# Decoder trunk on one core: softmax sums of a head's two attention units in one tile, guard on GpSimd, first query blocks turned together

## The chip, the cores and the metric

The kernel runs on one core of a Trainium2 chip. A core has five engines that run their own instruction streams and meet at semaphores: TensorE (in the profile PE, with its weight loads as PEld), VectorE (DVE), ScalarE (ACT), GpSimd (POOL) and SyncE (SP), which here issues the DMAs. The metric is the device time of one execution in microseconds; the median of three runs is 2022.24 us (2020.12 to 2023.56).

## The reference, cut to what matters

Two layers over 512 positions of width 1024, each a half-step SwiGLU, a token mixer, and another half-step SwiGLU, all with modulated norms. Layer 0's mixer is a short convolution beside latent attention with 8 heads. Layer 1's is sparse attention with 16 heads in three branches: compressed blocks, selected blocks, sliding window. With 512 positions the selection takes all 8 blocks and the window all positions, so that both branches are plain causal attention over 512 positions, each with its own keys and values:

```
def masked_softmax(s, mask):
    s = where(mask, s, NEG_INF)
    m = max(s, axis=-1)
    p = exp(s - m) * mask
    return p / maximum(sum(p, axis=-1), 1e-20)
...
o = gate0 * o_compressed + gate1 * o_selected + gate2 * o_window   # per head
```

The floor of 1e-20 under the sum is what this document calls the guard. The tensors are f32; products run as sums of products of a rounded high part and its remainder (`split`).

## The kernel before, in words

One program, unrolled: norms, feed-forward nets, and the two mixers one after another. The instructions of every engine stand in an order that a planner fixes when the program is built: it takes the order of the source as priority and lets an instruction pass others of its engine when, by its own costs, those aren't ready yet. At run time each engine's queue keeps that order, and an instruction whose operands are not ready holds what stands behind it.

Both mixers call `attend` (L512) with a list of units. A unit is one causal attention over 512 queries and keys: in layer 0 a head (8 units, `ahead=1`), in layer 1 a branch of a head (32 units; the selected branch has `ahead=2`, the window branch `ahead=0`). The queries of a unit go in four blocks of 128; block i sees (i+1) x 128 keys.

- `scores(n, i)` (L525): TensorE makes the scores of block i of unit n. VectorE adds the mask and takes the minimum in one operation (L547; the scores carry the opposite sign), with an operation that reads out the minimum. ScalarE exponentiates in place and sums (L549), with one that reads out the sum. After block 1 and after block 3, for the two blocks last made: the guard on the sums (L552, VectorE, 128x2), the reciprocal (L553, VectorE), and for each of the two blocks a multiplication by reciprocal and gate in place on GpSimd (L557). With `ahead=2` one pair of products makes block 0 of this unit and of the next, and the next unit then has no block 0 of its own. Minima, sums and reciprocals lie in a tile of four columns for each unit.
- `turn(n, i)` (L559): TensorE transposes block i (L565), and `split` puts the high part (ScalarE, L100) and the remainder (VectorE, L101) into `h`. Even units have the tiles 0 to 7 of `h`, odd units 8 to 15 (`ptile`, L856).
- `values(n)` (L569): the products of probabilities and values, into a bank of their own (L574); a unit that is the last of its head folds the two halves (L603, L604).

In pass n the loop at L580 calls: hook, scores(n, 0), scores(n, 1), turn(n-1, 0), scores(n, 2), turn(n-1, 1), values(n-2), scores(n, 3), turn(n-1, 2), turn(n-1, 3). The hook of layer 1 spreads the compressed branch over the passes, a quad of four heads at a time (L1048 to L1073), which is the period of the stage. `e` (blocks 1 to 3 of a unit) has two buffers, `e0` four, PSUM banks of tag A six.

Of the kernel before, what the change touches and what calls it, by code (L numbers as in the profile page):

```python
# [12 lines left out]
AF = mybir.ActivationFunctionType  # L13
OP = mybir.AluOpType
# [3 lines left out]
P = 128  # L18
# [12 lines left out]
class Net:  # L31
# [480 lines left out]
    def attend(self, units, hook, beside=iter(())):  # L512

        nc = self.nc
        live = {}

        def scores(n, i):  # L525
            u = units[n]
            w = (i + 1) * P
            qk, ahead = u["qk"], 1
            if i == 0:
                qk, ahead = u["first"] or qk, u["ahead"]  # L530
                for k in range(ahead):
                    live[n + k] = dict(e0=u["e0"](), mn=self.small(4), sum=self.small(4), r=self.small(4))
                if not ahead:
                    return
            L = live[n]
            if i == 1:
                L.update(e=u["e"](), pt=u["pt"](n))
            s = self.bank()
            for p, (q, k) in enumerate(qk):
                k = k[..., :w]  # L540
                nc.tensor.matmul(s[:, :ahead * w], q[:, i * P:(i + 1) * P], k, start=(p == 0),  # L541
                                 stop=(p == len(qk) - 1))
            for k in range(ahead):
                L = live[n + k]
                e = self.eblk(L, i)
                mn = L["mn"][:, i:i + 1]
                nc.vector.tensor_tensor_reduce(e, s[:, k * w:(k + 1) * w], self.cmask[:, S - w:], 1.0, 3e38, OP.add,  # L547
                                               OP.min, accum_out=mn)
                nc.scalar.activation(e, e, AF.Exp, bias=mn, scale=-1.0, accum_out=L["sum"][:, i:i + 1])  # L549
            if i % 2:  # L550
                c = slice(i - 1, i + 1)
                nc.vector.tensor_scalar(L["sum"][:, c], L["sum"][:, c], 1e-20, None, op0=OP.max)  # L552
                nc.vector.reciprocal(L["r"][:, c], L["sum"][:, c])  # L553
                for b in (i - 1, i):
                    g = 1.0 if u["gate"] is None else u["gate"](b)
                    eb = self.eblk(L, b)
                    nc.gpsimd.tensor_scalar(eb, eb, L["r"][:, b:b + 1], g, op0=OP.mult, op1=OP.mult)  # L557

        def turn(n, i):  # L559
            L = live[n]  # L560
            e = self.eblk(L, i)
            b = self.bank()
            w = (i + 1) * P
            for kb in range(i + 1):
                nc.tensor.transpose(b[:, kb * P:(kb + 1) * P], e[:, kb * P:(kb + 1) * P], self.ident)  # L565
            hi, lo = (t[:, 0:i + 1, i * P:(i + 1) * P] for t in L["pt"])
            self.split(b[:, :w].rearrange("p (k q) -> p k q", q=P), hi, lo)

        def values(n):  # L569
            u, L = units[n], live.pop(n)  # L570
            y, first = u["y"]()
            for kb in range(4):
                for p, t in enumerate(L["pt"]):
                    nc.tensor.matmul(y[:, kb * P:], u["v"](kb), t[:, kb, kb * P:], start=(first and kb == 0 and p == 0),  # L574
                                     stop=(u["last"] and kb == 3 and p == 1))
            if u["last"]:
                u["done"](y)

        N = len(units)
        for n in range(N + 2):  # L580
            hook(n)
            for i in range(5):
                if n < N and i < 4:
                    scores(n, i)
                if (n, i) in ((0, 1), (0, 3), (1, 1)):
                    next(beside, None)
                if 1 <= n <= N and i > 0:
                    turn(n - 1, i - 1)
                if n >= 2 and i == 2:
                    values(n - 2)  # L590

    def eblk(self, L, i):
        if i == 0:
# [632 lines left out]
```

## Time and profile before

| | |
|---|---|
| median of three runs | 2022.24 us (2020.12 to 2023.56) |
| the profiled execution: time, span | 2022.17 us, 2020.4 us |
| TensorE busy (granted clock 0.994 in the mean) | 1969.8 us, 97% |
| weight loads | 1659.3 us, 82% |
| VectorE busy | 1137.5 us, 56% |
| ScalarE busy | 765.7 us, 38% |
| GpSimd busy | 204.7 us, 10% |
| DMA | 248.06 MB, mean 123 GB/s |

The shares are means over stages with different limits. TensorE's busy time is modelled from pipelined instructions, so a TensorE that is busy all the time isn't one at its peak. The layer 0 attention lies at about 500 to 565 us, the layer 1 attention at about 1437 to 1597 us. The views below are the busy times by stretches, the groups by line and shape, the timeline, the waits, and the chain of waits that ended last.

### The profile page before, as it was taken

Reading aid. Unit: us, or ns where it says so; the run is one execution under the profiler, and the core shown is the slowest. Engines: PE = TensorE matmul, PEld = TensorE weight load, DVE = VectorE, ACT = ScalarE, POOL = GpSimd, SP = SyncE. Lnnn points to the kernel's source line nnn. Section 1 sums busy time; section 2 is a strip of 40 time slices with the busy share of each in tenths; the row PEclk is TensorE's granted clock in tenths of the full one; section 3 lists DMA queues with packets and bytes.
Section 4 is the critical chain, followed back from the end, with each engine's and each line's share of the span. In section 5 each row is a group of like instructions: output and inputs, shape, how many; then the busy total and the mean of one; then the engine's idle time right before and its main releaser. Section 6 shows DMA issues by size and latency. Waiting matters only on the chain. (4 is left out here: it accounts for less than half of the span.)

```text
span 2020.4 us, 26114 instructions
## 1 busy us (share of the span) xinstructions
PE 1969.8 (97%) x9990; PEld 1659.3 (82%) x9990; DVE 1137.5 (56%) x1993; ACT 765.7 (38%) x1372; POOL 204.7 (10%) x388
## 2 busy tenths in 40 slices
PE   6999999999999999999999999999999999999998
PEld 5788888897789888888988888889777798888887
DVE  7756566268756666663545443356799753333332
ACT  3322322245844223222422222236688643222223
POOL 3000000022400000000100000020355310000000
PEclk8999999999999999999999999999999999999999
DMA  9646666343114566664346452334200023333231
GB/s 277 195 134 206 190 205 206 84 100 94 43 53 126 177 193 206 192 207 139 108 122 177 126 153 87 96 97 119 62 1 2 22 74 115 94 95 99 88 97 49
DMA packets 374434, 248.06 MB, mean 123 GB/s; under 512 B 23207, under 2 KB 356262, under 8 KB 374310
## 3 DMA queue, kind: packets, MB, share of 16 engines
q1 hardware_dynamic: 373440, 245.24, 41.2%
q8 instruction: 78, 1.28, 0.3%
q10 hardware_dynamic: 870, 1.16, 0.2%
q14 instruction: 46, 0.38, 0.1%
HBM read 244.28 MB, written 2.10 MB: 122 GB/s over the span
## 5 line engine op out<-in xcount | busy, mean ns | idle before, releaser
L100 ACT ACTIVATE wh<-wr 128x1024 fp32r<-128x1024 f32 (+2 forms) x317 | 328.5, 1037 | 926.2 <-PE psA L126 388.0
L101 DVE TENSOR_TENSOR wl<-wr,wh 128x1024 fp32r<-128x1024 f32 (+2 forms) x317 | 379.7, 1200 | 396.4 <-ACT wh L100 390.6
L126 PE MATMUL psA<-h,wh 128*128 128x512 f32 (+1 forms) x1312 | 488.1, 372 | 1.0 <-DVE h L386 1.0
L127 PE MATMUL psA<-h,wl 128*128 128x512 f32 (+1 forms) x1312 | 488.6, 373 | 0.0
L125 PE MATMUL psA<-h,wh 128*128 128x512 f32 (+1 forms) x1312 | 485.0, 374 | 2.9 <-DVE mod L221 1.6
L126 PEld LDWEIGHTS psA<-h,wh 128*128 128x128 f32 x1312 | 247.4, 189 | 46.5 <-DVE h L386 1.7
L125 PEld LDWEIGHTS psA<-h,wh 128*128 128x128 f32 x1312 | 246.4, 189 | 46.6 <-issue 1.7
L127 PEld LDWEIGHTS psA<-h,wl 128*128 128x128 f32 x1312 | 247.2, 188 | 43.7
L125 PE MATMUL psY<-h,wh 128*128 128x512 f32 (+2 forms) x568 | 209.0, 368 | 0.0
L126 PE MATMUL psY<-h,wh 128*128 128x512 f32 (+2 forms) x568 | 208.5, 367 | 0.0
L127 PE MATMUL psY<-h,wl 128*128 128x512 f32 (+2 forms) x568 | 208.4, 367 | 0.0
L125 PE MATMUL psA<-g,wh 128*128 128x512 f32 (+1 forms) x528 | 192.7, 365 | 0.0
L126 PE MATMUL psA<-g,wh 128*128 128x512 f32 (+1 forms) x528 | 191.9, 363 | 0.0
L127 PE MATMUL psA<-g,wl 128*128 128x512 f32 (+1 forms) x528 | 191.6, 363 | 0.0
L279 DVE SCALAR_TENSOR_TENSOR acc<-wr,cact,acc 128x1024 f32<-128x1024 f32 x112 | 143.6, 1283 | 73.2 <-DMA wr<-in_ada_w 71.8
L351 POOL TENSOR_SCALAR s<-s 128x2 int32<-128x2 int32 (+1 forms) x14 | 5.1, 366 | 1534.1 <-ACT s L350 1534.0
L126 PEld LDWEIGHTS psY<-h,wh 128*128 128x128 f32 (+1 forms) x568 | 106.1, 187 | 18.5
L125 PEld LDWEIGHTS psY<-h,wh 128*128 128x128 f32 (+1 forms) x568 | 106.3, 187 | 18.1
L127 PEld LDWEIGHTS psY<-h,wl 128*128 128x128 f32 (+1 forms) x568 | 106.2, 187 | 17.9
L127 PEld LDWEIGHTS psA<-g,wl 128*128 128x128 f32 x528 | 99.7, 189 | 15.6
L126 PEld LDWEIGHTS psA<-g,wh 128*128 128x128 f32 x528 | 99.7, 189 | 15.5
L125 PEld LDWEIGHTS psA<-g,wh 128*128 128x128 f32 x528 | 99.7, 189 | 15.3
(274 smaller groups left out, 2596.5 us busy)
## 6 DMA issues: line engine op xcount, KB each, us to landing
wr<-in_ff_w SPq DMA_DIRECT2D x234, 512.0 KB, 4.6
wr<-in_ada_w SPq DMA_DIRECT2D x128, 512.0 KB, 4.2
wr<-in_ff_w SPq DMA_DIRECT2D x40, 384.0 KB, 3.0
ar<-in_ada_w SPq DMA_DIRECT2D x16, 512.0 KB, 5.8
wr<-in_hy_w_in SPq DMA_DIRECT2D x15, 512.0 KB, 3.9
wr<-in_nsa_w_in SPq DMA_DIRECT2D x14, 512.0 KB, 3.8
wr<-in_hy_w_out SPq DMA_DIRECT2D x8, 512.0 KB, 5.9
wr<-in_nsa_w_out SPq DMA_DIRECT2D x8, 512.0 KB, 3.6
```

The source lines that it names most:

```text
L100: nc.scalar.activation(hi, src, AF.Copy)
L101: (lo_eng or nc.vector).tensor_tensor(lo, src, hi.bitcast(F32), op=OP.subtract)
L125: mm(out, lh, rh, start=first, stop=False)
L126: mm(out, lh, rl, start=False, stop=False)
L127: self.product = mm(out, ll, rh, start=False, stop=last).ins
L279: nc.vector.scalar_tensor_tensor(acc, raw, self.cact[:, k:k + 1], acc, op0=OP.mult, op1=OP.add)
L351: pool.tensor_scalar(y.bitcast(I32), ms.bitcast(I32), -0.5, float(0x5F3759DF), op0=OP.mult, op1=OP.add)
```

## The change

- With `ahead=2` the two units of a head share tiles of eight columns for minima, sums and reciprocals. Block b of the first unit has column b + 1; of the second unit block 0 has column 0 and block b column b + 4.
- Guard, reciprocal and multiplications follow a table. In the sparse attention there are three runs a head: after block 1 of the first unit for its blocks 0 and 1 and the second unit's block 0 (columns 0 to 2); after block 3 of the first unit for its blocks 2 and 3; after block 3 of the second unit for its blocks 1, 2 and 3. The latent attention keeps its two runs a unit.
- The guard is issued on GpSimd, in both attentions.
- In the sparse attention the two first blocks of a head are transposed into one bank in the pass after the first unit's, and split with one copy and one subtraction into the tiles of both units.
- `values(n - 2)` stands ahead of `turn(n - 1, 0)` in pass n, after scores(n, 1), in both attentions.

```diff
@@ -528,8 +528,13 @@
             qk, ahead = u["qk"], 1
             if i == 0:
                 qk, ahead = u["first"] or qk, u["ahead"]
-                for k in range(ahead):
-                    live[n + k] = dict(e0=u["e0"](), mn=self.small(4), sum=self.small(4), r=self.small(4))
+                if ahead == 2:
+
+                    sh = {q: self.small(8, tag=q) for q in ("mn", "sum", "r")}
+                    live[n] = dict(sh, e0=u["e0"](), col=lambda b: b + 1)
+                    live[n + 1] = dict(sh, e0=u["e0"](), col=lambda b: b + 4 if b else 0)
+                elif ahead:
+                    live[n] = dict(e0=u["e0"](), mn=self.small(4), sum=self.small(4), r=self.small(4), col=lambda b: b)
                 if not ahead:
                     return
             L = live[n]
@@ -543,21 +548,36 @@
             for k in range(ahead):
                 L = live[n + k]
                 e = self.eblk(L, i)
-                mn = L["mn"][:, i:i + 1]
+                c = slice(L["col"](i), L["col"](i) + 1)
+                mn = L["mn"][:, c]
                 nc.vector.tensor_tensor_reduce(e, s[:, k * w:(k + 1) * w], self.cmask[:, S - w:], 1.0, 3e38, OP.add,
                                                OP.min, accum_out=mn)
-                nc.scalar.activation(e, e, AF.Exp, bias=mn, scale=-1.0, accum_out=L["sum"][:, i:i + 1])
-            if i % 2:
-                c = slice(i - 1, i + 1)
-                nc.vector.tensor_scalar(L["sum"][:, c], L["sum"][:, c], 1e-20, None, op0=OP.max)
+                nc.scalar.activation(e, e, AF.Exp, bias=mn, scale=-1.0, accum_out=L["sum"][:, c])
+
+            due = {(2, 1): [(n, 0), (n + 1, 0), (n, 1)], (0, 1): [], (0, 3): [(n, 1), (n, 2), (n, 3)]}
+            due = due.get((u["ahead"], i), [(n, i - 1), (n, i)] if i % 2 else [])
+            if due:
+                L = live[n]
+                cols = [live[m]["col"](b) for m, b in due]
+                c = slice(min(cols), max(cols) + 1)
+                nc.gpsimd.tensor_scalar(L["sum"][:, c], L["sum"][:, c], 1e-20, None, op0=OP.max)
                 nc.vector.reciprocal(L["r"][:, c], L["sum"][:, c])
-                for b in (i - 1, i):
-                    g = 1.0 if u["gate"] is None else u["gate"](b)
-                    eb = self.eblk(L, b)
-                    nc.gpsimd.tensor_scalar(eb, eb, L["r"][:, b:b + 1], g, op0=OP.mult, op1=OP.mult)
+                for (m, b), k in zip(due, cols):
+                    g = 1.0 if u["gate"] is None else units[m]["gate"](b)
+                    eb = self.eblk(live[m], b)
+                    nc.gpsimd.tensor_scalar(eb, eb, L["r"][:, k:k + 1], g, op0=OP.mult, op1=OP.mult)
 
         def turn(n, i):
             L = live[n]
+            if i == 0 and units[n]["ahead"] != 1:
+                if units[n]["ahead"]:
+
+                    b = self.bank()
+                    for k in range(2):
+                        nc.tensor.transpose(b[:, k * P:(k + 1) * P], live[n + k]["e0"], self.ident)
+                    self.split(b[:, :2 * P].rearrange("p (k q) -> p k q", q=P),
+                               *(self.h[:, s:s + 9:8, 0:P] for s in (0, 4)))
+                return
             e = self.eblk(L, i)
             b = self.bank()
             w = (i + 1) * P
@@ -584,10 +604,10 @@
                     scores(n, i)
                 if (n, i) in ((0, 1), (0, 3), (1, 1)):
                     next(beside, None)
+                if n >= 2 and i == 1:
+                    values(n - 2)
                 if 1 <= n <= N and i > 0:
                     turn(n - 1, i - 1)
-                if n >= 2 and i == 2:
-                    values(n - 2)
 
     def eblk(self, L, i):
         if i == 0:
```

## Rows read from the trace of the kernel before

**Rows 1.** Busy by stretch: window, us, PE, PEld, DVE, ACT, POOL; clock, DMA, GB/s.

```profile
...
500.00:550.00 50.00, 45.19 (x250) 37.69 (x248) 37.56 (x109) 36.92 (x90) 22.78 (x30) 1.00 0.19 53
...
1700.00:1750.00 50.00, 50.00 (x220) 41.01 (x220) 17.22 (x20) 14.81 (x20) 0.00 (x0) 1.00 0.33 95
```

**Rows 2.** The same view: one period of four heads, and the sparse attention's stage.

```profile
...
1463.75:1503.08 39.33, 36.59 (x230) 29.61 (x228) 38.28 (x146) 34.44 (x104) 21.68 (x36) 1.00 0.01 1
...
1447.00:1596.50 149.50, 138.72 (x864) 112.16 (x862) 143.82 (x544) 130.83 (x395) 82.11 (x133) 1.00 0.01 2
```

**Rows 3.** The chain of waits over two periods, shares by engine and line.

```profile
...
by line: DVE h L101 18.8%; DVE e L547 18.3%; ACT e L549 9.2%; POOL e L557 8.4%; issue 8.1%; DVE s L552 6.0%; PE psA L565 5.1%; PE psA L541 3.7%; DVE ys L604 3.5%; ACT h L100 3.4%; DVE y L101 3.3%; DVE s L553 2.9%; DVE s L1057 2.6%; PE psA L
```

**Rows 4.** Groups by shape, 1437 to 1597 us: count | busy us, mean ns | idle before.

```profile
...
L574 PE MATMUL psY<-h,vt 128*128 128x512 f32 x62 | 28.9, 471 | 3.5 <-DVE h L101 3.1
...
L557 POOL TENSOR_SCALAR e<-e,s,gates 128x256 f32<-128x256 f32 x32 | 17.7, 555 | 0.0
...
L552 DVE TENSOR_SCALAR s<-s 128x2 f32<-128x2 f32 x62 | 15.2, 245 | 2.7 <-ACT e L549 2.0
...
L101 DVE TENSOR_TENSOR h<-psA,h 128x256 fp32r<-128x256 f32 x32 | 13.2, 411 | 0.0
...
L553 DVE RECIPROCAL s<-s 128x2 f32<-128x2 f32 x62 | 9.5, 154 | 0.1
L101 DVE TENSOR_TENSOR h<-psA,h 128x128 fp32r<-128x128 f32 x32 | 9.0, 282 | 0.0
```

**Rows 5.** Timeline from 1479.67 us: start us, us, engine, line, operation [idle before <-releaser].

```profile
...
1479.67 1.41 POOL L557 TENSOR_SCALAR e<-e,s,gates 128x384 f32<-128x384 f32 x2 [1.58 <-DVE s L553]
...
1480.39 0.31 PEld L565 LDWEIGHTS psA<-ident,e 128*128 128x128 f32 x3 [0.34 <-POOL e L557]
...
1480.63 0.48 DVE L552 TENSOR_SCALAR s<-s 128x2 f32<-128x2 f32 x1
...
1481.35 0.15 DVE L553 RECIPROCAL s<-s 128x2 f32<-128x2 f32 x1
...
1481.67 0.98 POOL L557 TENSOR_SCALAR e<-e,s,gates 128x128 f32<-128x128 f32 x2 [0.59 <-DVE s L553]
...
1483.35 0.42 DVE L547 CUSTOM_DVE_ANT_0 e<-psA,cmask 128x256 f32<-128x256 f32 x1
...
1488.13 0.17 DVE L552 TENSOR_SCALAR s<-s 128x2 f32<-128x2 f32 x1
...
1488.21 0.68 DVE L101 TENSOR_TENSOR h<-psA,h 128x512 fp32r<-128x512 f32 x1
```

**Rows 6.** Who waited for whom, 1437 to 1597 us: us, times, longest.

```profile
...
POOL e L557 <- DVE s L553: 56.8, 39, 7.0
PEld psA L565 <- POOL e L557: 15.7, 41, 0.7
```

**Rows 7.** Groups by shape on GpSimd, whole span: small operations of the norms.

```profile
...
L362 POOL TENSOR_SCALAR s<-s 128x2 f32<-128x2 f32 x11 | 6.4, 582 | 1.0
...
L360 POOL TENSOR_SCALAR s<-s 128x2 f32<-128x2 f32 x11 | 2.1, 192 | 1.0
```

**Rows 8.** Timeline from 1465 us: one handover from ScalarE to GpSimd.

```profile
...
1468.73 0.62 ACT L1060 ACTIVATE ec<-ec 128x512 f32<-128x512 f32 x1
...
1469.43 0.46 POOL L1061 TENSOR_TENSOR ec<-ec,see 128x128 f32<-128x128 f32 x1 [2.11 <-ACT ec L1060]
```

**Rows 9.** The chain of waits in order of time: GpSimd's longest pieces in one period.

```profile
...
1474.49 1.42 POOL e L557 x2
...
1493.89 1.42 POOL e L557 x2
```

**Rows 10.** Timeline from 1465 us: first value product and the scores of block 2.

```profile
...
1477.70 0.48 PE L574 MATMUL psY<-h,vt 128*128 128x512 f32 x1
...
1478.02 0.51 PE L541 MATMUL psA<-key,q 128*128 128x384 f32 x2
```

**Rows 11.** Groups by shape, 500 to 600 us, latent attention: the guard.

```profile
...
L552 DVE TENSOR_SCALAR s<-s 128x2 f32<-128x2 f32 x16 | 3.3, 209 | 3.3 <-ACT e L549 3.2
```

## The prediction

> **What bounds the kernel now.** I read the table of busy time by stretches of 50 us first, to find where the changed code runs and which engine is full there. In the feed-forward nets TensorE is busy all 50 us, in the latent attention (from 500 us) 45.19 [rows 1], and in the sparse attention, where nearly all of the changed instructions are, 138.72 of 149.50 us; there VectorE is busy 143.82 [rows 2]. The finer table cuts this stage at its own period, four heads of two units each: 39.33 us, of which VectorE has 38.28, TensorE 36.59, ScalarE 34.44, GpSimd 21.68 [rows 2]. The reader is to see that one head takes 9.8 us with VectorE idle for 0.26 of it: whatever shortens VectorE's list can be handed on until TensorE, with 2.74 us of shown idle in a period, or a latency stops it. The chain of waits over two periods says the same by lines: VectorE's lead (splits 18.8%, masked minima 18.3%); the guard on the softmax sums (L552) has 6.0%, the reciprocal (L553) 2.9%, GpSimd's multiplication (L557) 8.4% [rows 3].
>
> The groups by shape give the prices. A guard is a 128x2 operation, yet it costs 245 ns in the mean, a reciprocal of the same shape 154 [rows 4]. The timeline shows why: one guard starts at 1480.63 and takes 0.48, to 1481.11, while two multiplications of GpSimd run from 1479.67 to 1481.08; where GpSimd is idle, at 1488.13, a guard takes 0.17 [rows 5]. So a guard that meets a multiplication stands until it ends, with VectorE's whole queue behind it. The waits show what else is late: GpSimd waits 56.8 us for reciprocals (39 times), TensorE's loads 15.7 us (41 times) for GpSimd's products [rows 6].
>
> **The change part by part.** Durations overlap on VectorE: the guard of 0.17 us at 1488.13 has the next operation behind it at 1488.21 [rows 5]. About 0.09 us of an operation is shared with the next, and I price what VectorE gets back by durations less 0.09.
>
> *Guards leave VectorE.* 62 of 64 are in the window: 15.2 us [rows 4], less 62 x 0.09 = 9.6 us. The chain of waits, independently, has 6.0% of its time there: 6.0% of 149.5 = 9.0 us. I take 9.0.
>
> *Three reciprocals a head instead of four.* 16 fewer: between 16 x 0.154 = 2.5 us and 16 x (0.154 - 0.09) = 1.0 us; by the chain a quarter of 2.9% of 149.5 = 1.1 us. I take 1.1.
>
> *The first query blocks of both units split together.* Two ScalarE copies and two VectorE subtractions 128x128 become one each of 128x256. On VectorE 2 x 282 - 411 = 153 ns, less a shared 0.09, is 0.06 us, in 16 heads 1.0 us [rows 4]; I count half, since the splits' chain is not on VectorE throughout: 0.5 us. On ScalarE the copies get fewer by as much, but it has 4.9 us of a period to spare [rows 2]: nothing. The transposes stay 20 a head and TensorE's work does not change.
>
> Released: 9.0 + 1.1 + 0.5 = 10.6 us. With the full releases, 9.6 + 1.4 + 1.0, it would be 12.0; TensorE's shown idle, 149.5 - 138.7 = 10.8 us [rows 2], is no tighter. These are the limits of the gain.
>
> *Guards arrive on GpSimd.* Small GpSimd operations of this shape take 192 ns, in the worst group 582 [rows 7]; 48 of them cost 9.2 to 28 us of an engine that has 17.6 us free in every period, so its load is covered and only the path counts. The path gains a handover. ScalarE to GpSimd is 0.08 us (1469.35 to 1469.43 [rows 8]), VectorE to GpSimd 0.17 (1481.50 to 1481.67 [rows 5]); GpSimd to VectorE is not read, I use 0.17. New: 0.08 + 0.19 + 0.17 = 0.44 us from exponential to reciprocal. Now: 0.17, and 0.04 ahead of it by estimate, half the handover to GpSimd. Each run is then 0.23 us later, 0.62 with the worst group. The reciprocal waits on VectorE for GpSimd, and the next unit's minima and splits stand behind it. The chain passes through GpSimd in three places of a period (8.4% of 39.3 is 3.3 us: two of 1.42 and a short one [rows 3, 9]), so 3 x 3.8 periods x 0.23 = 2.6 us; at the ends 0 (always covered) and 47 x 0.23 = 10.8 us.
>
> *A head's second unit has its block 1 multiplied with blocks 2 and 3.* The product of 128x256 (555 ns [rows 4]) moves from the run after block 1 to the run after block 3, where it stands ahead of the two larger ones. They come 0.56 us later, and block 1's transposes, so far ready, become as late as those of block 2, for which TensorE already waits (0.34 us at 1480.39 [rows 5]). 16 x 0.555 = 8.9 us at most, 0 at least. The products of 1.42 us on the chain start at 1474.49 and 1493.89 [rows 9]; both belong to a head's first unit, whose blocks 2 and 3 keep their run. The second unit's, at 1479.67 [rows 5], are not on it. I take a quarter: 2.2 us.
>
> *Value products ahead of the turns.* They need the last split of their unit, and by the written order a score pair and the turns would no longer lie between. But already the first value product starts at 1477.70, ahead of the scores at 1478.02 [rows 10]: the run order is nearly the new one. Bounds: their 3.5 us of TensorE idle [rows 4] gone, or 31 x 0.4 = 12 us more, a score pair's 0.51 us [rows 10] less its overlap. I take 0.
>
> *The latent attention* shares the guard's move and the earlier value products: 16 guards of 209 ns, 3.3 us [rows 11]. VectorE is busy 37.56 of 50 there [rows 1], so I count no gain; lost are at most 16 x 0.23 = 3.7 us. I take 0.
>
> Sum: -10.6 + 2.6 + 2.2 = -5.8 us. The profiled execution took 2022.17 us (span 2020.4), 0.07 under the median shown, so 2022.17 - 5.8 = 2016.4 us.
>
> **The rivals.**
>
> *The freed time counts in full* (B1). GpSimd mostly stands ready when a guard comes, since it waits for reciprocals 39 times [rows 6], and what is given back is covered: -12.0, 2010.2 us. Against it: TensorE already waits for products 41 times.
>
> *VectorE waits instead of working* (B2). The reciprocal holds VectorE until GpSimd's guard is done, 0.23 us more in each of 47 runs: 10.8 us of new delay against 10.6 released, so 2022.4. For it: the guard can find GpSimd amid 1.41 us of products [rows 5]. Against it: between guard and reciprocal another operation often stands already, as at 1483.35 [rows 5], and covers that.
>
> *The two engines stay in each other's way* (B4). A guard on GpSimd is held by VectorE as VectorE's guard is held now, the 9.0 us are nothing, and -1.6 + 4.8 gives 2025.4 us. The trace has the holding in one direction, 0.48 us against 0.17 for VectorE's guard [rows 5]; GpSimd's small operations have 192 ns and, in one group, 582 [rows 7]. The Trainium skill has this as a rule: its page "Perfetto Trace Analysis", section "Optimizing Scalar/DVE Operations", says that VectorE and GpSimd share a read port, so that offloading between the two might not help. The trace agrees as to the sharing, but the party that stands is the guard, and on GpSimd it would only queue behind the products of its own engine.
>
> *GpSimd's run of three limits a head's second unit* (B3, slower). After block 3, TensorE waits for guard, reciprocal and the product of block 1 ahead of the two larger. If both delays are on the path in every head, it is 8.9 + 10.8 = 19.7 us against 10.6: 9.1 us more, 2031.3; it decides from 10.6 / 16 = 0.66 us of added wait a head. For it: TensorE waits for these products today. Against it: VectorE is ahead by the 0.66 us that a head releases, and a late turn leaves TensorE the next scores.
>
> **How the numbers follow.** This kernel can be told from no change by about 0.2%, 4 us: faster is under 2018.2, slower over 2026.3. Forecast 0.52 (own range 2012 to 2021), B1 0.17, B2 0.11, B4 0.04, B3 0.16. Three quarters of the forecast's own case lie under 2018.2: 0.39, with B1's 0.17 faster has 0.56; the rest of it, B2 and B4 make 0.28 for the same, B3 0.16 for slower. The range starts at 2009, just under B1, and ends at 2026, which leaves out most of B3 and little else.
>
> **What would show it.** The period, now 39.3 us, should be 37.6 to 38 (10.6 - 4.8 us over 3.8 periods take 1.5 off). No guard on VectorE; 48 in the sparse attention and 16 in the latent one on GpSimd, of about 0.2 us. VectorE's idle time ahead of reciprocals should stay under 0.2 us in the mean; over 0.4 is B2, guards of over 0.4 us are B4. TensorE's loads waiting for products, 15.7 us, may grow by some 5; over 25 us in all is B3. VectorE's busy time in the stage should fall by 10 to 12 us. The forecast is wrong if the period stays, or if time moves outside the two attentions, where the change has no instruction.

## The result and the profile after

The changed kernel takes 2041.24 us (median of four runs, 2039.54 to 2042.54), beside 2022.76 for the kernel before in the same runs: 1.0089 times the time [1.0076, 1.0102], 18.5 us slower. The forecast was 2016.4 with a range of 2009 to 2026. The profiled execution took 2042.54 us with a span of 2040.8 us, 20.4 more than the span before.

The first reading is where the 20.4 us lie. The sparse attention's stage, from the first operation of its compressed branch on VectorE to the last copy of a head's half (`yl`), took 179.2 us before and 186.9 after: 7.7 us. The other 12.7 us are outside it, most of them in stretches in which the change has no instruction. The table of busy time by stretches of the changed kernel (columns as in [rows 1]) has both: a stretch of a feed-forward net's down products, and one period of four heads, which answers to the first of [rows 2].

```profile
...
870.00:930.00 60.00, 60.00 (x261) 48.40 (x260) 33.07 (x39) 13.46 (x16) 0.00 (x0) 1.00 0.65 197
1489.29:1530.32 41.03, 37.07 (x229) 30.93 (x228) 35.66 (x123) 34.12 (x100) 24.75 (x47) 0.96 0.00 1
...
```

The same stretch of the feed-forward net in the kernel before:

```profile
...
870.00:930.00 60.00, 60.00 (x268) 49.73 (x267) 33.96 (x43) 14.01 (x16) 0.00 (x0) 1.00 0.65 196
...
```

TensorE is busy for all 60 us at full clock in both, but after it gets 261 products done, before 268 (two and four of them small ones of 32 columns, the others of 512). From the start of one 512-column product from `g` to the start of the next the mean over the whole trace is 233.0 ns after and 227.1 before. Busy time can't show this: a slower product only makes the engine "busy" for longer. The count beside it does.

In the attention the period is 41.03 us against 39.33. VectorE's busy time in it fell from 38.28 to 35.66, as wanted, and the period grew all the same. The chain of waits over the stage is now led by GpSimd's multiplication (L568, before L557), where VectorE led before [rows 3]; among its pieces in order of time the run of three, 1.96 us, comes back twice a period:

```profile
...
by line: POOL e L568 14.9%; PE psY L594 13.1%; PE psA L585 9.6%; ACT e L555 9.3%; PE psA L546 9.0%; issue 6.8%; ACT h L100 5.5%; DVE h L101 4.0%; DVE e L553 3.8%; PE psA L125 3.3%; PE psA L126 3.2%; PE psA L127 3.2%; ACT yl L623 2.6%; POOL 
...
1489.29 1.96 POOL e L568 x3
...
1509.62 1.96 POOL e L568 x3
...
1530.32 1.96 POOL e L568 x3
...
```

The waits of the stage (1437 to 1620 us: total us, times, longest), which answer to [rows 6], show a new one, VectorE's reciprocal for GpSimd's guard:

```profile
...
PEld psA L585 <- POOL e L568: 15.7, 29, 2.2
POOL e L568 <- DVE r L564: 14.5, 42, 0.7
DVE r L564 <- POOL sum L563: 14.1, 21, 1.5
...
PEld psA L577 <- POOL e L568: 5.2, 16, 0.7
...
```

Groups by shape of the stage after (to be held against the L552 and L553 of [rows 4]): guards, reciprocals, the joint split's transposes.

```profile
...
L563 POOL TENSOR_SCALAR sum<-sum 128x3 f32<-128x3 f32 x32 | 7.1, 221 | 51.0 <-ACT e L555 51.0
...
L564 DVE RECIPROCAL r<-sum 128x3 f32<-128x3 f32 x32 | 5.6, 174 | 13.3 <-POOL sum L563 12.7
L577 PEld LDWEIGHTS psA<-ident,e 128*128 128x128 f32 x32 | 4.5, 147 | 5.2 <-POOL e L568 5.2
...
L563 POOL TENSOR_SCALAR sum<-sum 128x2 f32<-128x2 f32 x16 | 3.5, 219 | 2.8 <-ACT e L555 2.8
...
L564 DVE RECIPROCAL r<-sum 128x2 f32<-128x2 f32 x16 | 2.6, 165 | 2.2 <-POOL sum L563 1.5
```

A guard on GpSimd is cheap, 221 ns. But the 48 reciprocals have 13.3 + 2.2 = 15.5 us of VectorE's idle time ahead of them, where it was 0.1 us; the guards, then on VectorE, had 2.7 us ahead of them [rows 4]. The timeline shows how one of these waits comes about (start, us, engine, line, operation, idle before):

```profile
...
1488.69 0.22 POOL L563 TENSOR_SCALAR sum<-sum 128x3 f32<-128x3 f32 x1 [1.55 <-ACT e L555]
...
1488.94 0.18 DVE L564 RECIPROCAL r<-sum 128x3 f32<-128x3 f32 x1
...
1489.29 1.96 POOL L568 TENSOR_SCALAR e<-e,r,gates 128x256 f32<-128x256 f32 x3 [0.39 <-DVE r L564]
...
1491.22 0.22 POOL L563 TENSOR_SCALAR sum<-sum 128x3 f32<-128x3 f32 x1
...
1491.47 0.18 DVE L564 RECIPROCAL r<-sum 128x3 f32<-128x3 f32 x1 [1.13 <-POOL sum L563]
...
1491.75 0.46 POOL L568 TENSOR_SCALAR e<-e,r,gates 128x128 f32<-128x128 f32 x1 [0.31 <-DVE r L564]
```

The next head's guard stands in GpSimd's queue behind the run of three until 1491.22. VectorE has reached the reciprocal and stands idle for 1.13 us; then GpSimd waits 0.31 us for the reciprocal.

### The profile page after: what moved, and what is told of

It reads as the page before. It is cut to its first block, busy times and chain, and to the rows that moved or that the text cites. A ratio compares the mean times of both kernels' runs of the same rounds, so it can differ in the third digit from the quotient of the medians.

```text
span 2040.8 us, 26006 instructions
## 1 busy us (share of the span) xinstructions
PE 1983.7 (97%) x9990; PEld 1663.5 (82%) x9990; DVE 1124.7 (55%) x1881; ACT 764.9 (37%) x1356; POOL 221.7 (11%) x452
## 5 line engine op out<-in xcount | busy, mean ns | idle before, releaser
L125 PE MATMUL psA<-g,wh 128*128 128x512 f32 (+1 forms) x528 | 194.7, 369 | 0.0
L126 PE MATMUL psA<-g,wh 128*128 128x512 f32 (+1 forms) x528 | 194.0, 367 | 0.0
L125 PEld LDWEIGHTS psY<-h,wh 128*128 128x128 f32 (+1 forms) x568 | 106.7, 188 | 18.3
L127 PEld LDWEIGHTS psY<-h,wl 128*128 128x128 f32 (+1 forms) x568 | 106.5, 187 | 18.3
```

The costliest lines, as they stand in the source:

```text
L125: mm(out, lh, rh, start=first, stop=False)
L126: mm(out, lh, rl, start=False, stop=False)
L127: self.product = mm(out, ll, rh, start=False, stop=last).ins
```

## Experiments

Each run was timed beside the kernel before on the same chip; "x us slower" is the difference of the medians.

**1. Is it the attention, or the place of the tiles?** The eight-column tiles are three tags of four buffers of 32 bytes: `sm` grows by 384 bytes a partition, and every scratch pool allocated behind it, that of the feed-forward net's hidden values `g` among them, moves by as much. The first kernel gives the kernel before such tiles and uses them for nothing else; the second is the whole change with these tiles in a pool of the attention, so that `g` stays.

```diff
 pad_before (against before, ahead of the memset of cm in the sparse attention)
+        for q in ("mn", "sum", "r"):
+            nc.gpsimd.memset(self.small(8, tag=q), 0.0)
 after_moved (against after)
-                    sh = {q: self.small(8, tag=q) for q in ("mn", "sum", "r")}
+                    sh = {q: u["sh"](q) for q in ("mn", "sum", "r")}
...
+                        sh=lambda t: pool.tile([P, 8], F32, name=f"{t}8", tag=f"{t}8", bufs=4),
```

> The kernel before, with the change's three groups of eight-column tiles (4 buffers of 32 bytes each, 384 bytes a partition) set aside in the same pool and filled once, and nothing else of the change. Theory A (address): the pool's growth moves every later tile by 384 bytes, and with it the down products' moving operand g; in the trace after the change 512-column products from g go 217 to 50 us in place of 223, 230 ns each in place of 224. Then this kernel has 230 ns too and takes 2032 to 2035 us, 10 to 12 us over the kernel before, with the sparse attention's period at 39.3 us. Rival B: the slower products come from the attention's new order (clock or memory traffic carried over); then the products stay at 224 ns and the time within 2 us of the kernel before.

> The changed kernel with the three groups of eight-column tiles in the sparse attention's own pool, so that the feed-forward nets' tiles lie where they lay before. Theory A (address): the down products are back at 224 ns and the time is 2028 to 2031 us, 10 to 12 us under the changed kernel; what stays over the kernel before, 6 to 9 us, belongs to the attention. Rival B: no part of the loss comes from where the tiles lie; 2039 to 2043 us.

pad_before: 2033.70 us, 1.0061 [1.0046, 1.0076], 11.9 us slower with no work added but three small memsets. Its stage takes 179.6 us, as before (179.2); all the loss is outside. after_moved: 2032.59, 1.0053 [1.0036, 1.0070], a little above what was expected; its time outside the stage is 1.5 us above that of before, in the stage it has 185.7 us. So the place of the tiles explains the part outside the attention, and the attention's loss is another matter, 10.7 us by after_moved's median. The two add to 22.6 where 18.5 were measured; the intervals (9.3 to 15.4 and 7.3 to 14.2) allow for the difference. The traces put the attention lower: the stage is 7.7 us longer in the changed kernel and 6.5 in after_moved, whose profiled execution was the fastest of its four (2030.12). The length of the stage is the steadier measure: in the six kernels that leave the attention as it was (before, pad_before, g_64, g_128, all_384, h_place) it is 178.4 to 179.6 us. By stretches, pad_before, then after_moved:

```profile
...
870.00:930.00 60.00, 60.00 (x260) 48.45 (x259) 32.37 (x38) 13.21 (x15) 0.00 (x0) 1.00 0.66 197
...
```

```profile
...
870.00:930.00 60.00, 60.00 (x268) 49.74 (x267) 32.41 (x41) 14.01 (x16) 0.00 (x0) 1.00 0.62 190
...
1480.92:1521.53 40.61, 36.38 (x229) 29.33 (x228) 35.53 (x123) 34.25 (x100) 24.63 (x48) 1.00 0.00 1
```

The changed kernel's period had a granted clock of 0.96, that of after_moved 1.00 with a period only 0.4 us shorter and still 1.3 us over that of before; the clock is not the main cause.

**2. Which place counts?** `h` and `wh`, `wl` (rounded weights and remainder) lie ahead of `sm`, `g` behind it. Three kernels add padding and nothing else.

```diff
 g_64, g_128 (16 or 32 columns; ahead of the memset of cm)
+        nc.gpsimd.memset(self.sm.tile([P, 16], F32, name="pad", tag="pad", bufs=1), 0.0)
 all_384 (ahead of x, so that h, the weights and g all move)
+        nc.vector.memset(c.tile([P, 96], F32, name="pad0"), 0.0)
```

> The kernel before with 64 bytes a partition set aside ahead of g, which then starts 192 past a multiple of 256, as h does. If the place within 256 bytes decides: products from g as those from h, 226 ns, about 4 us slower than the kernel before. If only a move by a multiple of 128 counts: 224 ns and no change.

> The kernel before with 128 bytes a partition set aside ahead of g, which then starts at a multiple of 256, as in the changed kernel. If the place within 256 bytes decides: 230 ns for a product from g, 10 to 12 us slower than the kernel before. If the change's slower products come from the move by 384 as such: another rate than 230 ns.

> The kernel before with 384 bytes a partition set aside ahead of x, h, the weights and g, which move all together. If g's own place decides: 230 ns a product from g and 10 to 12 us slower, before what the move does to h. If g's place relative to the weights decides, which stays: 224 ns, and h's 226 ns too.

One execution each: 2023.97, 2034.93 and 2020.95 us (before, there: 2024.46), so that the counts carry the argument and not the times; g_64 doesn't show the 4 us that its slower products would cost. In all_384 `g` has the same absolute remainder modulo 256 bytes as in the changed kernel, and its products are as fast as before; the weights moved with it. So the start of the moving operand relative to the weights counts, and not the absolute one. The raw weights and the temporaries of 512 columns lie in pools between `h` and `sm`, in buffers of a multiple of 256 bytes, and move with the weights in all these kernels; which of the three `g` has to agree with isn't separated. `g` and `h` in the table are these starts modulo 256 bytes; the counts are products done in 870 to 930 us (from `g`) and in 150 to 250 us (from `h`), two or four small ones of 32 columns among them:

| kernel | g less weights | from g, in 60 us | h less weights | from h, in 100 us |
|---|---|---|---|---|
| before | 0 | 268 | 64 | 440 |
| after | 128 | 261 | 64 | 440 |
| pad_before | 128 | 260 | 64 | 441 |
| after_moved | 0 | 268 | 64 | 440 |
| g_64 | 64 | 266 | 64 | 441 |
| g_128 | 128 | 260 | 64 | 440 |
| all_384 | 0 | 268 | 64 | 440 |
| h_place (below) | 0 | 268 | 0 | 444 |

g_64's row, then all_384's:

```profile
...
870.00:930.00 60.00, 60.00 (x266) 49.27 (x264) 32.76 (x43) 14.03 (x16) 0.00 (x0) 1.00 0.64 194
...
```

```profile
...
870.00:930.00 60.00, 60.00 (x268) 49.72 (x267) 33.22 (x42) 14.02 (x16) 0.00 (x0) 1.00 0.60 181
...
```

The groups by shape show the same in one of the six groups of products from `g`, before and then pad_before:

```profile
...
L125 PE MATMUL psA<-g,wh 128*128 128x512 f32 x396 | 154.5, 390 | 0.0
...
```

```profile
...
L125 PE MATMUL psA<-g,wh 128*128 128x512 f32 x396 | 156.7, 396 | 0.0
...
```

The kernel has 3 x (396 + 220) = 1848 products of 512 columns from `g`. From start to start they take 227.1 ns before, 229.1 in g_64 and 233.2 in pad_before; 6.1 ns each is 11.3 us, against the 11.9 of pad_before. (The 224, 226 and 230 ns of the expectations divide a stretch by all of its products, small ones included.)

**3. The attention, one part at a time.** The guard on GpSimd alone, the guard left out, and the early value products alone, each against before.

```diff
 guard_only
-                nc.vector.tensor_scalar(L["sum"][:, c], L["sum"][:, c], 1e-20, None, op0=OP.max)
+                nc.gpsimd.tensor_scalar(L["sum"][:, c], L["sum"][:, c], 1e-20, None, op0=OP.max)
 no_guard
-                nc.vector.tensor_scalar(L["sum"][:, c], L["sum"][:, c], 1e-20, None, op0=OP.max)
 values_early
+                if n >= 2 and i == 1:
+                    values(n - 2)
                 if 1 <= n <= N and i > 0:
                     turn(n - 1, i - 1)
-                if n >= 2 and i == 2:
-                    values(n - 2)
```

> The kernel before with the guard on GpSimd and nothing else of the change. Prediction's term: 9.0 us released on VectorE less the handover (0.23 us for each of the places where the chain passes through GpSimd, here 16 a period), so 2014 to 2020 us, with the period near 38 us. Rival B2 (VectorE's reciprocal waits for GpSimd's guard): 2021 to 2026 us, with idle time of VectorE ahead of reciprocals of over 0.3 us in the mean and a period of 39.3 us or more.

> The kernel before without the guard: the floor of 1e-20 under the softmax sums is left out in both attentions, nothing takes its place on GpSimd. Prediction's term by itself: VectorE's 9.0 us on the chain are handed on in full, with no handover: 2011 to 2015 us and a period near 37 us. Rival C (TensorE's order and its waits set the period, VectorE's fullness is only shown): VectorE's busy share falls by 7% as with the guard on GpSimd, yet the period stays at 39 us or more and the time at 2019 to 2024 us.

> The kernel before with the value products ahead of the turns and nothing else of the change. Prediction's term: 0, the planner's order was nearly this one already: within 2 us of the kernel before. Rival: the value products stand in TensorE's queue waiting for the split of the last block with nothing to cover it: 4 to 12 us slower, TensorE's waits of the value products for the split up from 14 us to 20 or more in the sparse attention, and a period of 40.5 us or more.

guard_only: 2027.47 us, 1.0029 [1.0019, 1.0038], 5.6 slower, above both ranges. no_guard: 2017.90, 0.998 [0.9970, 0.9989], 4.5 faster, between the two ranges. values_early: 2025.19, 1.0015 [1.0006, 1.0024], 3.3 slower, between what the two theories gave. Their stages take 184.3, 176.7 and 180.9 us (179.2 before). The periods, guard_only, then no_guard:

```profile
...
1464.29:1504.23 39.94, 36.65 (x229) 29.72 (x229) 36.16 (x129) 34.56 (x106) 25.81 (x52) 1.00 0.01 1
...
```

```profile
...
1460.16:1498.72 38.56, 36.45 (x230) 29.63 (x229) 35.89 (x130) 34.52 (x105) 22.05 (x36) 1.00 0.01 1
...
```

These two rows are the core of the case. In both, VectorE has lost its guards: 2.1 and 2.4 us of busy time a period. Without the guard the period falls by 0.8 us only, a third of that; with the guard on GpSimd it grows by 0.6. So VectorE at 38.28 of 39.33 us was not the whole limit, and the way over GpSimd costs 1.4 us a period, more than all that was to be had. Where no_guard's time then goes is seen in its chain of waits over two periods, by line: ScalarE's exponential (L549) leads, and VectorE's lines have fallen (splits 18.8 to 13.1%, minima 18.3 to 8.4% [rows 3]).

```profile
...
by line: ACT e L549 18.0%; DVE h L101 13.1%; PE psY L573 11.1%; ACT h L100 10.0%; issue 9.0%; DVE e L547 8.4%; DVE ys L603 5.3%; PE psA L541 4.9%; PE psA L564 4.2%; POOL ec L1057 4.1%; ACT yl L602 3.6%; DVE s L1056 2.3%; PE psY L1084 1.9%; 
...
```

And of guard_only over two periods, the groups of the guard and the reciprocal:

```profile
...
L552 POOL TENSOR_SCALAR s<-s 128x2 f32<-128x2 f32 x32 | 6.6, 207 | 19.2 <-ACT e L549 19.1
...
L553 DVE RECIPROCAL s<-s 128x2 f32<-128x2 f32 x32 | 5.3, 165 | 5.1 <-POOL s L552 3.7
...
```

VectorE gives 5.1 us in 32 reciprocals back as idle time. That is 0.16 us in the mean, where B2 had asked for over 0.3: the mechanism is B2's, smaller a time, and the loss is larger than B2's range all the same. That later products for all who wait behind them make up the rest of the 10.1 us between no_guard and guard_only is an argument; no single row shows it.

In values_early TensorE's idle time ahead of the value products is no longer than before (3.1 us, 3.5 before). What grew is the guards' time on VectorE, 282 ns in the mean from 245 [rows 4]. That this is the loss is likely and not shown; no run separates it from the new order. From 1447 to 1600 us:

```profile
...
L552 DVE TENSOR_SCALAR s<-s 128x2 f32<-128x2 f32 x62 | 17.5, 282 | 1.5 <-ACT e L549 1.2
...
```

**4. The parts that are left.** Against after_moved: guard on VectorE; four runs a head; joint split undone and value products at their old place; guard left out.

```diff
 moved_vguard
-                nc.gpsimd.tensor_scalar(L["sum"][:, c], L["sum"][:, c], 1e-20, None, op0=OP.max)
+                nc.vector.tensor_scalar(L["sum"][:, c], L["sum"][:, c], 1e-20, None, op0=OP.max)
 moved_runs4
-            due = {(2, 1): [(n, 0), (n + 1, 0), (n, 1)], (0, 1): [], (0, 3): [(n, 1), (n, 2), (n, 3)]}
+            due = {(2, 1): [(n, 0), (n + 1, 0), (n, 1)], (0, 1): [(n, 1)]}
 moved_single
-            if i == 0 and units[n]["ahead"] != 1:
...
-                return
...
-                if n >= 2 and i == 1:
-                    values(n - 2)
...
+                if n >= 2 and i == 2:
+                    values(n - 2)
 rest_noguard
-                nc.gpsimd.tensor_scalar(L["sum"][:, c], L["sum"][:, c], 1e-20, None, op0=OP.max)
```

> The changed kernel with its eight-column tiles in the attention's own pool, as in the run after_moved (2032.6 us), and the guard back on VectorE. If the handover through GpSimd costs in the changed kernel what it cost alone (5.6 us): 2025 to 2029 us, VectorE's idle time ahead of reciprocals gone from 6.6 us in two periods to under 1. Rival: the run of three and the joint split set the time; 2031 to 2035 us.

> As after_moved (2032.6 us), with four runs a head: the second unit's block 1 gets its own guard, reciprocal and product after block 1. Rival B3 of the prediction (the run of three makes the second unit's blocks late): 2026 to 2030 us, TensorE's loads waiting for products under 10 us in two periods, and the chain no longer through three products of 1.95 us. If the run of three costs nothing: one guard and one reciprocal a head more, 2032 to 2035 us.

> As after_moved (2032.6 us), with the first query blocks turned one by one again and the value products back behind the second turn; guard on GpSimd and three runs a head stay. If the early value products and the joint split cost as the value products did alone (3.3 us): 2027 to 2031 us, TensorE's idle time ahead of value products down from 5.6 us in two periods to under 2.5. Rival: their cost is swallowed by the guard's; 2031 to 2034 us.

> The changed kernel with its eight-column tiles in the attention's own pool, as after_moved (2032.6 us), and without a guard (the floor of 1e-20 under the softmax sums is left out). If the rest of the change were worth what the prediction released for it (1.6 us less 2.2 us): 2017 to 2020 us, as the kernel before without the guard (2017.9). If run of three and early value products cost by themselves: 2023 to 2030 us, a period of 39.8 us or more in place of 38.6.

| kernel | median, us | ratio to before | less before, us | stage, us |
|---|---|---|---|---|
| after_moved | 2032.59 | 1.0053 [1.0036, 1.0070] | +10.7 | 185.7 |
| moved_vguard | 2034.40 | 1.0058 [1.0043, 1.0073] | +12.0 | 189.9 |
| moved_runs4 | 2028.61 | 1.0029 [1.0018, 1.0040] | +6.2 | 185.5 |
| moved_single | 2027.84 | 1.0026 [1.0016, 1.0036] | +5.4 | 184.6 |
| rest_noguard | 2022.30 | 1.0000 [0.9990, 1.0009] | -0.8 | 180.2 |

By the medians the run of three costs 10.7 - 6.2 = 4.5 us, as its rival had it. But the intervals overlap (7.3 to 14.2 and 3.6 to 8.1), and the traces don't bear it out: with four runs a head the stage is as long as with three (185.5 and 185.7 us), and the period is longer, 41.10 us against 40.61 (four runs have a guard and a reciprocal a head more):

```profile
...
1471.77:1512.87 41.10, 37.63 (x229) 29.57 (x228) 36.09 (x125) 34.18 (x101) 25.46 (x51) 1.00 0.00 1
...
```

moved_single, which keeps the run of three beside the guard on GpSimd, is as fast as guard_only (+5.4 and +5.6). So no cost of the run of three is shown. Without a guard on either side the rest of the change loses the 4.5 us that no_guard wins, but for 0.8, between the two ranges expected; so the rest costs 3.7 (3.5 by the stage), and the guard on GpSimd 11.5 against none (10.1 in experiment 3). The stages, which leave out the latent attention's guards, have 5.5 and 7.6.

moved_vguard went with the rival: with its guards on VectorE the change is no faster than with GpSimd's, and its stage is 4.2 us longer. Against none, a guard on VectorE costs 12.8 us there, so that the 11.5 in the changed kernel can't be put down to the handover alone; for that the pair no_guard and guard_only stands. moved_vguard's groups by shape show guards in the sparse attention that are hardly held:

```profile
...
L564 DVE RECIPROCAL r<-sum 128x3 f32<-128x3 f32 x31 | 5.2, 169 | 0.2
L563 DVE TENSOR_SCALAR sum<-sum 128x3 f32<-128x3 f32 x31 | 5.2, 168 | 5.2 <-ACT e L555 4.5
...
```

168 ns against 245 before. That led to a guess: in two of the three runs the first column of the sums is odd, and perhaps such a guard isn't held by GpSimd. What remains open is why the kernel with these cheap guards is no faster.

**5. Odd columns, and a better kernel.** odd_columns moves the sums one column on, in the kernel before. h_place pads before `x` and behind `h`, so that `h` also starts where the weights do, modulo 256 bytes (`x` moves by as much as `h`); odd_h is both, noguard_h is h_place without the guard.

```diff
 odd_columns
-                nc.scalar.activation(e, e, AF.Exp, bias=mn, scale=-1.0, accum_out=L["sum"][:, i:i + 1])
+                nc.scalar.activation(e, e, AF.Exp, bias=mn, scale=-1.0, accum_out=L["sum"][:, i + 1:i + 2])
...
+                o = slice(i, i + 2)
+                nc.vector.tensor_scalar(L["sum"][:, o], L["sum"][:, o], 1e-20, None, op0=OP.max)
+                nc.vector.reciprocal(L["r"][:, c], L["sum"][:, o])
 h_place
+        nc.vector.memset(c.tile([P, 48], F32, name="pad0"), 0.0)
         self.x = c.tile([P, KD, S], F32, name="x")
         self.h = c.tile([P, 2 * KD, S], R, name="h")
+        nc.vector.memset(c.tile([P, 16], F32, name="pad1"), 0.0)
```

> The kernel before with the sums in columns 1 to 4 of a tile of eight, so that the guard's two columns start at an odd one (4 or 12 bytes into the tile); guard on VectorE, nothing else moved. In moved_vguard 48 guards of three columns, or of two from an odd one, took at most 319 ns, while 16 of two from an even column took up to 1122. If the column decides whether the guard waits for GpSimd: mean 165 to 175 ns in place of 245, and 2017 to 2020 us. If that was a matter of when they came: mean 230 ns or more and 2021 to 2024 us.

> The kernel before with 192 bytes a partition ahead of x and h and 64 behind h, so that h lies a multiple of 256 bytes from the weights, as g does. By noguard_h against no_guard (7.3 us less): 2013 to 2017 us, 445 products from h in 100 us in place of 440. If the gain there hung on the missing guard: 2020 to 2024 us.

> odd_columns and h_place together, nothing of the computation left out. If both count and add: 2009 to 2013 us. If the odd columns count for nothing: 2013 to 2017 us, as h_place.

> The kernel without the guard (run no_guard, 2017.9 us; the floor under the softmax sums is left out), with 192 bytes a partition set aside ahead of x and h and 64 behind h, so that h starts at 128 past a multiple of 256 bytes as g does in the kernel before; g and the weights keep their place to the multiple of 256. If the place within 256 bytes sets the rate of products (g at 128: 224 ns for 512 columns, at 0: 230; h at 192: 226): products from h go 223 to 50 us in place of 221, and the time is 2006 to 2012 us. If the place isn't what h's 226 ns come from: 2016 to 2020 us.

odd_columns: 2022.78 us, 1.0001 [0.9990, 1.0012]. Its guards take 246 ns, as before; the guess falls, which leaves when the guards come. The timeline bears that out: 28 of moved_vguard's 32 guards of three columns start while GpSimd is idle, before it was 34 of 64. Whether three columns in place of two matter as well, no run tests. The guards of odd_columns:

```profile
...
L554 DVE TENSOR_SCALAR s<-s 128x2 f32<-128x2 f32 x62 | 15.2, 246 | 2.7 <-ACT e L550 2.0
...
```

h_place: 2015.98 us, 0.9970 [0.9959, 0.9982], 7.1 faster; odd_h: 2015.15, 0.9965 [0.9952, 0.9978]; noguard_h: 2010.61, 0.9930 [0.9907, 0.9952]. All three beat both kernels. h_place leaves nothing out and needs two pads. By stretches, before and then h_place, where `h` is the moving operand:

```profile
...
150.00:250.00 100.00, 100.00 (x440) 82.14 (x439) 61.23 (x72) 28.72 (x35) 0.00 (x0) 1.00 0.66 201
...
```

```profile
...
150.00:250.00 100.00, 100.00 (x444) 82.80 (x444) 60.70 (x72) 30.45 (x37) 0.00 (x0) 1.00 0.66 201
...
```

## Why the prediction was wrong, point by point

**The step that failed first: the sum held only what the diff's lines do.** The forecast counted no time outside the two attentions and named it as what would make it wrong. 11.9 of 18.5 us came from there, by the tiles' place in memory (pad_before, after_moved; by the traces 12.7 of 20.4). The diff shows the cause, three tags of eight columns in a pool that lies ahead of `g`; I read it as three tiles and not as 384 bytes.

**Guards leave VectorE, -9.0: mis-sized.** The busy time went as forecast (35.66 from 38.28 us a period, 10 us over 3.8 periods). But the guard left out altogether is worth 4.5 us in both attentions, 2.5 of it in the stage that the 9.0 were counted for (176.7 us from 179.2). The share of a line in the chain of waits is what it holds now, not what comes out when it goes: the exponentials and the splits' copies on ScalarE and the value products stood close behind, and took the chain over.

**Guards arrive on GpSimd, +2.6: the largest miss inside the attention,** 10.1 us by no_guard and guard_only, near the upper end of 10.8 that I kept for the range (7.6 by the stage alone). The price of a guard was right (0.19 us assumed, 0.21 to 0.22 measured). The number of places was wrong: I charged the handover where GpSimd was already on the chain, three a period, while VectorE waits for the guard all over the period. That 10.1 is close to 47 runs at 0.23 us is no confirmation: guard_only has four runs a head, and its reciprocals wait 0.16 us in the mean. Part of the price is another thing, a guard behind GpSimd's own products (1.13 us at 1491.47). B2 named the mechanism and gave it 10.8; its 2022.4 was too low because it set the full 10.6 against it and, like the forecast, had nothing outside the attentions. In the changed kernel the mean idle time ahead of a reciprocal came to 15.5 / 48 = 0.32 us, between my two marks of 0.2 and 0.4.

**B4, that guards on GpSimd are held by VectorE, is wrong:** it needed guards of over 0.4 us, and they took 221 and 219 ns. The Trainium skill's page "Perfetto Trace Analysis", section "Optimizing Scalar/DVE Operations", says that offloading between VectorE and GpSimd might not help, for they share a read port. It did not help, by 5.6 us, but what the rows show is reciprocals that wait for the handover and for GpSimd's queue; none shows GpSimd's guards held by a port.

**The second unit's block 1 with blocks 2 and 3, +2.2:** not shown to cost anything; 4.5 us by medians whose intervals overlap, 0.2 by the stage. B3's place was right: GpSimd's multiplications lead the chain and the runs of three are its longest pieces, but with four runs a head the period is no shorter. TensorE's loads waited 15.7 + 5.2 = 20.9 us for products, about the 5 us of growth I allowed, under B3's mark of 25. B3's 2031.3 is close to after_moved's 2032.59 by luck: it had 10.6 us coming back from VectorE, of which 4.5 or less did.

**Value products ahead of the turns, 0:** 3.3 us alone, inside the bounds of -3.5 to +12. TensorE's wait, by which I bounded it, hardly changed (3.5 to 3.1 us); that guards on VectorE would be held for longer was in none of my terms, and with the guard on GpSimd it can't be the cost in the changed kernel.

**Three reciprocals and the joint split, -1.6:** not measured apart. (The 1.4 us for the reciprocals in the full release of 12.0 isn't derived; the working gives 1.0 to 2.5.) **The latent attention, 0:** from the first residual sum (`x<-psA,half`) of the net ahead of it to its own first (`x<-psA,mod`) there are 257.1 us before and 257.5 in after_moved. The zero holds as a sum of two parts: without a guard (no_guard) there are 255.5, so the guard's move to GpSimd takes back there what leaving VectorE gives.

What stays open: why only a third of VectorE's freed time comes back, why moved_vguard is no faster than after_moved, which part of the rest of the change makes its 3.7 us, and how much of the attention's 6.5 to 10.7 us each part has, since the parts don't simply add.

## What to carry to other kernels

Before pricing a change, work out what its tiles move: a pool that grows by some bytes shifts everything behind it, and a matmul-bound stage elsewhere can pay more than the change is about. Compare products done per stretch, not busy shares, in stages that the change doesn't touch. An engine busy for 97% of a period need not be the whole limit: 2.4 us of its work left out gave 0.8 us here. Leave the operation out once and time that, before paying for a handover to another engine's queue.

## What was unexpected of the hardware

With no work changed but the memsets of the pads, the rate of TensorE's 512-column f32 products depended on where the moving operand starts relative to the weights, modulo 256 bytes. From the start of one product to the start of the next, in the mean over a trace, `g` took 227.1 ns at 0 (before), 229.1 at 64 (g_64) and 233.2 at 128 (pad_before), and `h` 229.8 ns at 64 (before) against 227.6 at 0 (h_place). A move of 384 bytes of operand and weights together did not matter (all_384: 227.1). Other distances weren't tried, and the cause isn't known from these runs.
